# A two-layer attention trunk on one core: the last output tile in two halves, and six fp32 low parts moved between GpSimd and VectorE

## The chip, the core and the metric

The kernel runs on one core of a Trainium2 chip. The core has five engines with a queue each, worked off in order: TensorE (PE in the profile; its weight loads are PEld), VectorE (DVE), ScalarE (ACT), GpSimd (POOL) and SyncE (SP), which here issues the transfers. The metric is the device time of one execution in microseconds; the time of a kernel is the median of its runs.

## The reference

Two layers of one trunk, d_model 1024, on 512 latent tokens and 256 context tokens, in fp32:

```python
def _layer(x, ctx, ...):
    hx = _rmsnorm(x, norm_g) * (1.0 + scale_x) + shift_x      # the same for the context
    a_k, a_v, b_k, b_v, a_q, b_q, a_z, b_z, g_a, g_b = _split(hx @ w_in, SPLIT_SIZES)
    a_att = _na_latent(qa, ka, va, cka, cva, rpb, rows)       # 8 heads, 8 x 16 window + all context
    b_att = _gqa_latent(qb, k_all, v_all)                     # 8 query heads, 2 key heads, all tokens
    out_x = _merge(...)
    return x + gate_x * out_x, ctx                            # layer 0 updates ctx in the same way

def _merge(a_att, b_att, a_z, b_z, g_a, g_b, w_o_a, w_o_b, w_out):
    o_a = (a_att * jax.nn.silu(a_z)) @ w_o_a
    o_b = (b_att * jax.nn.silu(b_z)) @ w_o_b
    merged = jax.nn.sigmoid(g_a) * o_a + jax.nn.sigmoid(g_b) * o_b
    return merged @ w_out
```

`qa`, `ka`, `qb`, `kb` are the normalised (and, for b, rotated) queries and keys of 64 per head. Only the 512 latent tokens of layer 1 are returned, so layer 0 works on 768 tokens throughout and layer 1 on 512 wherever the context is not read.

## The kernel before

**Products in three matmuls.** Each fp32 operand is split into a high part (the value rounded to the format fp32r) and a low part (the value minus its high part, again in fp32r). A product is then three matmuls of 128 rows and up to 512 columns (`mm3`, L351 to L353: high x high, high x low, low x high). The high parts are casts on ScalarE (`whi`, `gah`), the low parts subtractions on VectorE or GpSimd (`wlo`, `gal`). Weights come by DMA from HBM in tiles 128x512 (`raw`) and are split as they come, by `load_w` (L324 makes `wlo`) or `load_w2` (L338). Which engine makes the low part of weight tile k is a rule that the caller hands in; the usual one is

```python
    mix_lo = lambda k: V if k % 2 == 1 else G
```

with V for VectorE and G for GpSimd.

**Stages of a layer.** After the normalisation the keys, the values (`load_w(W, C_AV, ...)`, L621) and the queries of branch a are projected, tile by tile of 128 tokens, with `tok_proj` (PSUM tiles `psx`); the keys' tiles are normalised after it: sums of squares (`ss`, L415, VectorE), their scale (`rsa`, `rsb`, L285 and L287, GpSimd), the scaled tile (`y`, L419, VectorE), and four transposes of it by TensorE (L431). Then come the two attentions, first the windowed one (a), then the grouped one (b). A block of attention b runs as a pipeline over the heads: scores (`pss`, L718 and L719, TensorE), row maximum (`mx`, L955, VectorE), exponential (ScalarE), reciprocal and scaling by it (`r`, `p`, L653 to L659, VectorE and GpSimd), transposes of the probabilities (`pst`, L669, TensorE), their high and low parts (`pth` L672, ScalarE; `ptl` L673, VectorE), the product with the values (`psv`, L972 and L973, TensorE) and the head's output (`ho`, L682, VectorE).

**Filling.** Softmax would leave TensorE waiting, so pieces of other projections are placed between the steps of attention: the gates' pieces (stored through ScalarE's `zt`, L516, as `gs`), and, as soon as branch a is through, its output projection, `o_chunks("a", ...)`. Such a piece is 12 matmuls into one PSUM buffer `psf`, after which VectorE folds it into the gate tile `tg` (L592). Its operand is the gated tile of branch a (`za`, attention times SiLU). Its split into `gah` and `gal` is made by `hilo` in four parts, at the first filling piece of that projection:

```python
        def hilo(src, dst, fs):
            sv = src.rearrange("p (f n) -> p f n", f=4)
            for f in fs:
                S.copy(R(dst[0][:, f, :ntok]), sv[:, f, :ntok])
                G.tensor_tensor(R(dst[1][:, f, :ntok]), sv[:, f, :ntok], dst[0][:, f, :ntok], ALU.subtract)
```

Line L557 is the cast and L558 the subtraction; a part is 128x768 in layer 0 and 128x512 in layer 1. `prepare` (L579) calls it for branch a.

**The end.** Both branches are merged (`mh`, `ml`: high and low part of the merged tile), and the last projection runs in two halves of 512 output columns, each over four (layer 1) tiles of 128 tokens, 24 matmuls a tile. `evac_o` (L1036) then multiplies the tile by the gate (`t`, L1039, from PSUM), adds it to the residual (`xt`, L1041), both on VectorE, and in layer 1 sends the 256 KB to HBM.

**What sets the order.** The program is written stage by stage, and a scheduler that simulates engines with costs of its own orders the instructions on each engine before the kernel is built; on the chip each engine then keeps that order. PSUM has eight buffers: in attention b one `psf`, two `pst`, one `psv` and two `pss` of two banks. Nothing that the change touches has an order written by hand, except the values' weights of layer 0, where the rule was VectorE alone already.

Of the kernel before, what the change touches and what calls it, by code (L numbers as in the profile page):

```python
# [8 lines left out]
F32 = mybir.dt.float32  # L9
# [49 lines left out]
def R(ap):  # L59
    return ap.bitcast(F32R)  # L60
# [7 lines left out]
def hybrid_kernel(es: ExitStack, tc, x, ctx, cvec, w_ada, w_ada0, small, gvec, w_in, w_o_a, w_o_b, w_out,  # L68
# [13 lines left out]
    def nm(s):  # L82
        uid[0] += 1
        return f"{s}_{uid[0]}"
# [405 lines left out]
    def layer(l, hx, nxt, mid):  # L490
# [60 lines left out]
        def hilo_tiles(name):  # L551
            return [big(name + part).rearrange("p (f n) -> p f n", f=4) for part in "hl"]

        def hilo(src, dst, fs):
            sv = src.rearrange("p (f n) -> p f n", f=4)
            for f in fs:
                S.copy(R(dst[0][:, f, :ntok]), sv[:, f, :ntok])  # L557
                G.tensor_tensor(R(dst[1][:, f, :ntok]), sv[:, f, :ntok], dst[0][:, f, :ntok], ALU.subtract)  # L558

        def load_tg(c):  # L560
            nc.sync.dma_start(tg[c].rearrange("p (f n) -> p f n", f=4)[:, :, :ntok], gs[c][:, :, :ntok])
# [17 lines left out]
        def prepare():  # L579

            gated["a"] = hilo_tiles("ga")
            hilo(za, gated["a"], range(4))
            for c in (0, 2):
                tg[c] = big("tg")
                load_tg(c)
# [32 lines left out]
        per_bg = -(-len(bg) // (2 + qt))  # L618
        va = [big("va0"), big("va1")]
        at = len(nc.cur_bb.bb.instructions)  # L620
        w = load_w(W, C_AV, 512, KT, (lambda k: V) if first else mix_lo)  # L621
        if first:
            in_program_order((ON_DVE, ON_ACT), nc.cur_bb.bb.instructions[at:], start_last)
        for t in range(6):
# [370 lines left out]
        with tc.tile_pool(name=f"mrg{l}", bufs=1, reuse_waits="tile") as mp:  # L995
# [37 lines left out]
            for n in range(2):  # L1033
                w = load_w(w_out[l], 512 * n, 512, KT, mix_lo)

                def evac_o(t, ps, n=n):  # L1036
                    cs = slice(512 * n, 512 * n + 512)
                    t1 = mp.tile([128, 512], F32, tag="t1", name=nm("t1"), bufs=2)
                    V.tensor_tensor(t1, ps, gv[:, 0 if t < 4 else 1, cs], ALU.mult)  # L1039
                    xt = xts[t]  # L1040
                    V.tensor_tensor(xt[:, cs], xt[:, cs], t1, ALU.add)  # L1041
                    if not first:
                        nc.sync.dma_start(o_lat[16 * t:16 * t + 16][:, :, cs], xt[:, cs])
                    elif n == 1:
                        if t < 4:
                            nc.sync.dma_start(xs1[128 * t:128 * t + 128, :], xt)
                        late.append(lambda: make_hx(1, t, xt, nxt(), mp))
                late = []
                for t in range(nt):
                    tok_proj(w, 512, a_m, t, evac_o)  # L1050
                    run(bg, per_bg)
                    run(late, len(late) - 1)
                run(late, len(late))
# [186 lines left out]
```

## Time and profile before

| | |
|---|---|
| median of 3 runs | 1148.73 us (1148.03 to 1149.26) |
| the profiled execution | 1149.07 us, of which the span is 1147.0 us |
| TensorE busy | 1123.5 us, 98% of the span |
| VectorE busy | 818.3 us, 71% |
| ScalarE busy | 580.3 us, 51% |
| GpSimd busy | 483.0 us, 42% |
| DMA | 118 GB/s on average |

The first line is the metric. The second is the one execution that was traced: its span runs from the first to the last record, and all starts and durations of rows are counted from its beginning. A busy time is a sum over the records of an engine. A row of the timeline gives start, duration, engine, line, operation, output and inputs, shape, the count of equal neighbours that were drawn together, and in brackets the idle time of the engine before it and what ended it. The first filling piece of branch a's output projection stands at about 480 us in layer 0 and 1005 us in layer 1, the values' weights of layer 1 at about 693 us.

### The profile page before, as it was taken

The page shows a single profiled execution, that of the slowest core. Times are in us where ns is not written, and L with a number is a line of the kernel's source. Part 1 is how long each engine was busy: PE and PEld are TensorE (multiplying, and loading weights), DVE is VectorE, ACT ScalarE, POOL GpSimd, SP SyncE. Part 2 cuts the span into 40 slices and gives each one's busy share as a digit, 9 for nine tenths or more (in the row PEclk, how much of TensorE's full clock was granted, in tenths as well). Part 3 has the DMA queues.
Part 4 walks back from the last instruction along what each step waited for, and adds up shares of the span by engine and source line. Part 5 has one row for each costly group of instructions (what it writes and reads, how often), then busy time and mean ns, then how long its engine had stood idle before and what let it go on. Part 6 is the DMA issues. An engine that isn't in the chain of part 4 may idle for free.

```text
span 1147.0 us, 17434 instructions
## 1 busy us (share of the span) xinstructions
PE 1123.5 (98%) x6136; PEld 949.2 (83%) x6136; DVE 818.3 (71%) x1533; ACT 580.3 (51%) x1185; POOL 483.0 (42%) x449
## 2 busy tenths in 40 slices
PE   7999999999999999999999999999999999999998
PEld 5788888888988888888788787888888888887786
DVE  6777688997454786697588755469787665898563
ACT  6553366655433565665330355336666355766421
POOL 1073355453374343453411227345554664465311
PEclk9999999999999999999999999999999999999999
DMA  9645311333322232451434424633332333152143
GB/s 370 232 127 156 90 51 60 105 110 111 106 101 89 95 103 92 92 221 38 149 127 130 151 70 122 193 89 115 97 113 74 111 102 101 65 176 90 61 133 92
DMA packets 89695, 135.08 MB, mean 118 GB/s; under 512 B 10789, under 2 KB 52745, under 8 KB 88969
## 3 DMA queue, kind: packets, MB, share of 16 engines
q1 hardware_dynamic: 89328, 133.87, 36.8%
q8 instruction: 48, 0.79, 0.3%
q14 instruction: 39, 0.31, 0.1%
q10 hardware_dynamic: 280, 0.12, 0.0%
HBM read 116.63 MB, written 17.32 MB: 117 GB/s over the span
## 4 chain that ended last, share of the span: by engine, by line
PE 80%; DVE 7%; DMA 4%; issue 3%; ACT 3%; POOL 2%; SPq 0%; POOLq 0%; ACTq 0%; DVEq 0%
PE psx L353 12%; PE psx L352 12%; PE psx L351 11%; PE psf L351 9%; PE psf L352 9%; PE psf L353 9%; PE pst L669 4%; DMA raw<-in_w_in_dram 2%; PE pss L718 2%; PE pss L719 2%; PE psv L973 2%; PE psv L972 1%; PE pss L795 1%; PE pst L431 1%; DMA rawb<-in_w_ada_dram 1%
## 5 line engine op out<-in xcount | busy, mean ns | idle before, releaser
L673 DVE TENSOR_TENSOR ptl<-pst,pth 128x512 fp32r<-128x512 f32 (+1 forms) x176 | 115.9, 671 | 46.4 <-ACT pth L672 45.4
L672 ACT CAST pth<-pst 128x512 fp32r<-128x512 f32 (+1 forms) x176 | 99.3, 577 | 86.7 <-PE pst L669 55.8
L338 POOL TENSOR_TENSOR wlo<-raw,whi 128x512 fp32r<-128x512 f32 x68 | 95.6, 1409 | 105.1 <-ACT whi L336 83.9
L351 PE MATMUL psf<-hx,whi 128*128 128x512 f32 (+1 forms) x368 | 139.2, 378 | 0.6 <-ACT zt L516 0.6
L352 PE MATMUL psf<-hx,whi 128*128 128x512 f32 (+1 forms) x368 | 138.2, 375 | 0.0
L353 PE MATMUL psf<-hx,wlo 128*128 128x512 f32 (+1 forms) x368 | 137.8, 374 | 0.0
L351 PE MATMUL psx<-whi,hx 128*128 128x512 f32 (+1 forms) x368 | 137.6, 375 | 0.0
L353 PE MATMUL psx<-whi,hx 128*128 128x512 f32 (+1 forms) x368 | 135.9, 369 | 0.1
L352 PE MATMUL psx<-wlo,hx 128*128 128x512 f32 (+1 forms) x368 | 135.7, 369 | 0.0
L336 ACT CAST whi<-raw 128x512 fp32r<-128x512 f32 x136 | 82.7, 621 | 51.6 <-DMA raw<-in_w_in_dram 35.6
L321 ACT CAST whi<-raw 128x512 fp32r<-128x512 f32 x88 | 53.9, 623 | 99.6 <-PE psx L353 38.1
L669 PE MATMUL pst<-ident,p 128*128 128x128 f32 x640 | 99.9, 272 | 1.4 <-DVE ptl L673 0.8
L324 POOL TENSOR_TENSOR wlo<-raw,whi 128x512 fp32r<-128x512 f32 x36 | 50.9, 1416 | 110.0 <-ACT whi L321 74.6
L338 DVE TENSOR_TENSOR wlo<-raw,whi 128x512 fp32r<-128x512 f32 x68 | 68.6, 1010 | 28.1 <-ACT whi L336 27.2
L669 PEld LDWEIGHTS pst<-ident,p 128*128 128x128 f32 x640 | 77.8, 140 | 13.0 <-DVE ptl L673 1.3
L658 POOL TENSOR_SCALAR r<-r 128x1 f32<-128x1 f32 x64 | 22.4, 350 | 152.2 <-DVE r L653 145.2
L659 POOL TENSOR_TENSOR p<-p,r 128x512 f32<-128x512 f32 (+1 forms) x64 | 84.2, 1316 | 5.1
L353 PEld LDWEIGHTS psx<-whi,hx 128*128 128x128 f32 x368 | 69.4, 189 | 12.6 <-DVE hx L1137 1.0
L351 PEld LDWEIGHTS psx<-whi,hx 128*128 128x128 f32 x368 | 69.5, 189 | 12.4 <-issue 0.8
L353 PEld LDWEIGHTS psf<-hx,wlo 128*128 128x128 f32 x368 | 69.4, 188 | 11.8
L351 PEld LDWEIGHTS psf<-hx,whi 128*128 128x128 f32 x368 | 69.4, 189 | 11.4 <-ACT zt L516 0.8
L352 PEld LDWEIGHTS psx<-wlo,hx 128*128 128x128 f32 x368 | 69.5, 189 | 10.8
(252 smaller groups left out, 3056.0 us busy)
## 6 DMA issues: line engine op xcount, KB each, us to landing
raw<-in_w_in_dram SPq DMA_DIRECT2D x168, 256.0 KB, 2.9
rawb<-in_w_ada_dram SPq DMA_DIRECT2D x64, 256.0 KB, 2.9
gs<-zt SPq DMA_DIRECT2D x32, 256.0 KB, 2.1
raw<-in_w_out_dram SPq DMA_DIRECT2D x32, 256.0 KB, 2.9
tg<-gs SPq DMA_DIRECT2D x4, 1536.0 KB, 6.8
rawx<-in_w_ada_dram SPq DMA_DIRECT2D x8, 512.0 KB, 7.9
raw<-in_w_o_a_dram SPq DMA_DIRECT2D x16, 256.0 KB, 2.8
raw<-in_w_o_b_dram SPq DMA_DIRECT2D x16, 256.0 KB, 2.8
```

The costliest lines, as they stand in the source:

```text
L321: S.copy(hi[:, :n], raw[:, :n])
L324: e.tensor_tensor(lo[:, :n], raw[:, :n], F(hi[:, :n]), ALU.subtract)
L336: S.copy(hi, raw)
L338: lo_eng(i).tensor_tensor(lo, raw, F(hi), ALU.subtract)
L351: T.matmul(ps, lhs[0], rhs[0], start=first, stop=False)
L352: T.matmul(ps, lhs[0], rhs[1], start=False, stop=False)
L353: T.matmul(ps, lhs[1], rhs[0], start=False, stop=last)
L659: G.tensor_tensor(p[:, c0:c1], p[:, c0:c1], r[:, i:i + 1].to_broadcast([128, c1 - c0]), ALU.mult)
L669: T.transpose(pt[:, c0:c0 + 128], src, ident)
L672: S.copy(hi[:, n0:n1], pt[:, n0:n1])
L673: V.tensor_tensor(lo[:, n0:n1], pt[:, n0:n1], F(hi[:, n0:n1]), ALU.subtract)
L718: T.matmul(ps[:, c0:c0 + n], q, sl(kh), start=True, stop=False)
```

## The change

Three edits:

- `hilo` takes a list of engines and deals the four subtractions out by turns. Only branch a's call hands one in, (VectorE, GpSimd): in each layer parts 0 and 2 of the gated tile's low half go to VectorE, parts 1 and 3 stay on GpSimd. Branch b's calls are as before.
- The values' weights of layer 1 have all eight low parts on VectorE; four of them were on GpSimd.
- The last token tile of the last half of layer 1's last projection is computed in two parts of 256 columns, with a PSUM buffer, a multiply, an add and a transfer each.

```diff
--- before.py
+++ after.py
@@ -551,11 +551,11 @@
         def hilo_tiles(name):
             return [big(name + part).rearrange("p (f n) -> p f n", f=4) for part in "hl"]
 
-        def hilo(src, dst, fs):
+        def hilo(src, dst, fs, on=(G,)):
             sv = src.rearrange("p (f n) -> p f n", f=4)
             for f in fs:
                 S.copy(R(dst[0][:, f, :ntok]), sv[:, f, :ntok])
-                G.tensor_tensor(R(dst[1][:, f, :ntok]), sv[:, f, :ntok], dst[0][:, f, :ntok], ALU.subtract)
+                on[f % len(on)].tensor_tensor(R(dst[1][:, f, :ntok]), sv[:, f, :ntok], dst[0][:, f, :ntok], ALU.subtract)
 
         def load_tg(c):
             nc.sync.dma_start(tg[c].rearrange("p (f n) -> p f n", f=4)[:, :, :ntok], gs[c][:, :, :ntok])
@@ -579,7 +579,7 @@
         def prepare():
 
             gated["a"] = hilo_tiles("ga")
-            hilo(za, gated["a"], range(4))
+            hilo(za, gated["a"], range(4), (V, G))
             for c in (0, 2):
                 tg[c] = big("tg")
                 load_tg(c)
@@ -618,7 +618,7 @@
         per_bg = -(-len(bg) // (2 + qt))
         va = [big("va0"), big("va1")]
         at = len(nc.cur_bb.bb.instructions)
-        w = load_w(W, C_AV, 512, KT, (lambda k: V) if first else mix_lo)
+        w = load_w(W, C_AV, 512, KT, lambda k: V)
         if first:
             in_program_order((ON_DVE, ON_ACT), nc.cur_bb.bb.instructions[at:], start_last)
         for t in range(6):
@@ -1033,9 +1033,9 @@
             for n in range(2):
                 w = load_w(w_out[l], 512 * n, 512, KT, mix_lo)
 
-                def evac_o(t, ps, n=n):
-                    cs = slice(512 * n, 512 * n + 512)
-                    t1 = mp.tile([128, 512], F32, tag="t1", name=nm("t1"), bufs=2)
+                def evac_o(t, ps, n=n, c=(0, 512)):
+                    cs = slice(512 * n + c[0], 512 * n + c[1])
+                    t1 = mp.tile([128, 512], F32, tag="t1", name=nm("t1"), bufs=2)[:, :c[1] - c[0]]
                     V.tensor_tensor(t1, ps, gv[:, 0 if t < 4 else 1, cs], ALU.mult)
                     xt = xts[t]
                     V.tensor_tensor(xt[:, cs], xt[:, cs], t1, ALU.add)
@@ -1047,6 +1047,12 @@
                         late.append(lambda: make_hx(1, t, xt, nxt(), mp))
                 late = []
                 for t in range(nt):
+                    if not first and n == 1 and t == nt - 1:
+                        for c in ((0, 256), (256, 512)):
+                            ps = psw(256)
+                            tok_mm(ps, [[a[:, c[0]:c[1]] for a in x] for x in w], 256, a_m, t, 0, KT)
+                            evac_o(t, ps, c=c)
+                        break
                     tok_proj(w, 512, a_m, t, evac_o)
                     run(bg, per_bg)
                     run(late, len(late) - 1)
```

The edits name engines and a shape; the scheduler orders anew. Three places show what came of it. Numbers behind a name tell tiles of the same name apart; a + stands ahead of a row that is new at its place, a - ahead of one that left it.

VectorE, layer 0, at the first gated tile (`gal_1249`). `ptl` are the low parts of probabilities, `wlo_1307` a low part of weights:

```order
 L673 TENSOR_TENSOR ptl_1226_5535<-pst_1224_5529,pth_1225_5534 128x512
 L673 TENSOR_TENSOR ptl_1229_5546<-pst_1227_5540,pth_1228_5545 128x512
+L558 TENSOR_TENSOR gal_1249_5608<-za_230_1097,gah_1248_5607 128x768 x2
 L338 TENSOR_TENSOR wlo_1307_5843<-raw_1305_5839,whi_1306_5841 128x512
 L673 TENSOR_TENSOR ptl_1232_5557<-pst_1230_5551,pth_1231_5556 128x512
```

Two subtractions of 128x768 now stand ahead of `wlo_1307`, after two `ptl` of the running head.

VectorE a few rows on; `tg_1250` is the gate tile, folded with the first pieces `psf_1252` and `psf_1253`:

```order
 L673 TENSOR_TENSOR ptl_1235_5568<-pst_1233_5562,pth_1234_5567 128x512
+L592 SCALAR_TENSOR_TENSOR tg_1250_5617<-tg_1250_5617,psf_1252_5621 128x512
 L673 TENSOR_TENSOR ptl_1239_5583<-pst_1237_5577,pth_1238_5582 128x512
 L955 TENSOR_REDUCE mx_1266_5697<-pss_1264_5691 128x1
 L955 TENSOR_REDUCE mx_1270_5709<-pss_1268_5703 128x1
+L682 TENSOR_TENSOR ho_1236_5573<-psv_1217_5506,ho_1236_5573 64x512
+L673 TENSOR_TENSOR ptl_1279_5737<-pst_1277_5731,pth_1278_5736 128x512
+L592 SCALAR_TENSOR_TENSOR tg_1250_5617<-tg_1250_5617,psf_1253_5635 128x256
 L653 RECIPROCAL r_1267_5699<-r_1267_5699 128x1
-L592 SCALAR_TENSOR_TENSOR tg_1250_5617<-tg_1250_5617,psf_1252_5621 128x512
+L731 TENSOR_REDUCE mx_1273_5721<-pss_1272_5716 128x2
+L653 RECIPROCAL r_1271_5711<-r_1271_5711 128x1
```

The fold moved up, ahead of the reciprocals and maxima (`r`, `mx`) that it followed.

VectorE, layer 1, at the keys' norms; `wlo_1724` to `wlo_1733` belong to the values' weights, `ss8` and `y` to the norms of the keys' tiles:

```order
+L324 TENSOR_TENSOR wlo_1724_7801<-raw_1722_7797,whi_1723_7799 128x512
 L415 TENSOR_REDUCE ss8_1682_7587<-sq_1681_7585 128x8
 L415 TENSOR_REDUCE ss8_1688_7622<-sq_1687_7620 128x8
 L324 TENSOR_TENSOR wlo_1727_7807<-raw_1725_7803,whi_1726_7805 128x512
+L324 TENSOR_TENSOR wlo_1730_7813<-raw_1728_7809,whi_1729_7811 128x512
 L415 TENSOR_REDUCE ss8_1694_7657<-sq_1693_7655 128x8
 L415 TENSOR_REDUCE ss8_1701_7698<-sq_1700_7696 128x8
 L419 TENSOR_TENSOR y_1680_7584<-psx_1679_7559,rsb_1684_7591 128x512
+L324 TENSOR_TENSOR wlo_1733_7819<-raw_1731_7815,whi_1732_7817 128x512
 L415 TENSOR_REDUCE ss8_1708_7739<-sq_1707_7737 128x8
+L419 TENSOR_TENSOR y_1686_7619<-psx_1685_7594,rsb_1690_7626 128x512
```

A `wlo` now precedes the first two sums of squares and another the next two, both ahead of the first scaled tile `y_1680`.

GpSimd at the same place; `rsa` and `rsb` are the two steps of the norms' scale:

```order
 L287 TENSOR_TENSOR rsb_1648_7477<-rsa_1647_7475,ehalf_108 128x1
-L324 TENSOR_TENSOR wlo_1724_7801<-raw_1722_7797,whi_1723_7799 128x512
 L285 TENSOR_SCALAR rsa_1683_7589<-ss8_1682_7587 128x8
 L287 TENSOR_TENSOR rsb_1684_7591<-rsa_1683_7589,ehalf_108 128x8
 L285 TENSOR_SCALAR rsa_1689_7624<-ss8_1688_7622 128x8
-L324 TENSOR_TENSOR wlo_1730_7813<-raw_1728_7809,whi_1729_7811 128x512
+L287 TENSOR_TENSOR rsb_1690_7626<-rsa_1689_7624,ehalf_108 128x8
 L285 TENSOR_SCALAR rsa_1695_7659<-ss8_1694_7657 128x8
-L287 TENSOR_TENSOR rsb_1690_7626<-rsa_1689_7624,ehalf_108 128x8
```

The two subtractions are gone, and the second `rsb` moves up behind its own `rsa`.

TensorE in layer 1, the tail of attention b: first before, from the last of four transposes into `pst_2647` on. `psf_2710` is a piece of branch a's output projection, and these are the first seven of its 12 matmuls:

```order
L669 MATMUL pst_2647_11516<-ident_90,p_2595_11332 128x128
L351 MATMUL psf_2710_11767<-gah_2576_11259,whi_2665_11591 128x512
L352 MATMUL psf_2710_11767<-gal_2577_11260,whi_2665_11591 128x512
L353 MATMUL psf_2710_11767<-gah_2576_11259,wlo_2666_11593 128x512
L351 MATMUL psf_2710_11767<-gah_2576_11259,whi_2665_11591 128x512
L352 MATMUL psf_2710_11767<-gal_2577_11260,whi_2665_11591 128x512
L353 MATMUL psf_2710_11767<-gah_2576_11259,wlo_2666_11593 128x512
L351 MATMUL psf_2710_11767<-gah_2576_11259,whi_2668_11597 128x512
```

The same place after the change; `psf_2751` is the next piece, of branch b's projection, and `pss_2684` the last scores of attention b:

```order
L669 MATMUL pst_2647_11516<-ident_90,p_2595_11332 128x128
L351 MATMUL psf_2751_11903<-gbh_2713_11785,whi_2738_11879 128x512
L352 MATMUL psf_2751_11903<-gbl_2714_11786,whi_2738_11879 128x512
L353 MATMUL psf_2751_11903<-gbh_2713_11785,wlo_2739_11881 128x512
L351 MATMUL psf_2751_11903<-gbh_2713_11785,whi_2738_11879 128x512
L718 MATMUL pss_2684_11655<-gk_2198_9743,qs_2671_11615 128x512
L719 MATMUL pss_2684_11655<-gk_2198_9743,qs_2671_11615 128x512
L718 MATMUL pss_2684_11655<-gk_2198_9743,qs_2671_11615 128x256
L719 MATMUL pss_2684_11655<-gk_2198_9743,qs_2671_11615 128x256
```

Branch a's piece has moved ahead of this place, four matmuls of a later piece stand here instead, and the scores `pss_2684` follow directly.

VectorE at the same place; `mx`, `r`, `ptl` and `ho` belong to the last two heads, `wlo_2766` to the weights of a later projection:

```order
-L592 SCALAR_TENSOR_TENSOR tg_2579_11271<-tg_2579_11271,psf_2709_11753 128x512
+L592 SCALAR_TENSOR_TENSOR tg_2579_11271<-tg_2579_11271,psf_2710_11767 128x512
+L955 TENSOR_REDUCE mx_2678_11636<-pss_2676_11630 128x1
+L338 TENSOR_TENSOR wlo_2766_11993<-raw_2764_11989,whi_2765_11991 128x512
 L673 TENSOR_TENSOR ptl_2646_11511<-pst_2644_11505,pth_2645_11510 128x512
-L955 TENSOR_REDUCE mx_2678_11636<-pss_2676_11630 128x1
 L955 TENSOR_REDUCE mx_2682_11649<-pss_2680_11643 128x1
+L653 RECIPROCAL r_2679_11638<-r_2679_11638 128x1
 L682 TENSOR_TENSOR ho_2617_11407<-psv_2598_11340,ho_2617_11407 64x512
 L673 TENSOR_TENSOR ptl_2649_11522<-pst_2647_11516,pth_2648_11521 128x512
-L653 RECIPROCAL r_2679_11638<-r_2679_11638 128x1
+L955 TENSOR_REDUCE mx_2686_11661<-pss_2684_11655 128x1
```

Ahead of `ptl_2646` now stand the fold of the later piece, the maximum `mx_2678` and the weights' `wlo_2766`.

## The prediction

> **What bounds the kernel now.** I read the page's busy shares first, then busy time by stage for the stages that the edits touch, then the waits and the timeline inside them. The first line below is from the page, the others are stretches of the span; their columns are the length, then busy time and instruction count of each engine, the granted clock, the DMA share and GB/s.
>
> ```profile
> PE 1123.5 (98%) x6136; PEld 949.2 (83%) x6136; DVE 818.3 (71%) x1533; ACT 580.3 (51%) x1185; POOL 483.0 (42%) x449
> 480.00:504.00 24.00, 21.71 (x135) 18.47 (x134) 19.76 (x32) 16.63 (x33) 17.46 (x13) 1.00 0.84 315
> 690.00:712.00 22.00, 21.21 (x101) 17.09 (x100) 12.77 (x21) 13.38 (x26) 17.48 (x17) 1.00 0.39 116
> 1000.00:1048.00 48.00, 47.70 (x250) 39.62 (x250) 44.04 (x66) 32.51 (x63) 28.32 (x26) 1.00 0.43 148
> 1048.00:1080.00 32.00, 29.24 (x155) 21.98 (x155) 22.38 (x34) 17.94 (x33) 13.29 (x13) 1.00 0.16 50
> ```
>
> TensorE works 98% of the span, at a granted clock of 1.00, so an edit gains only where TensorE waits. In the four stretches it is short of the full time by 2.3, 0.8, 0.3 and 2.8 us: 6.2 us in all is what the two moves of work could give at most by these rows (short waits that hide behind the modelled end of a matmul come on top). In the third stretch VectorE is busy 44 of 48 us: it is nearly a second bound there, and what the change does there is put work on VectorE.
>
> **The end of the kernel.** The last tile's 24 matmuls of 512 columns become 48 of 256, with two multiplies, two adds and two output transfers.
>
> ```profile
> 1136.18 0.39 PE L352 MATMUL psx<-wlo,mh 128*128 128x512 f32 x1
> 1141.17 0.39 PE L353 MATMUL psx<-whi,ml 128*128 128x512 f32 x1
> 1141.60 0.69 DVE L1039 TENSOR_TENSOR t<-psx,gate 128x512 f32<-128x512 f32 x1 [3.80 <-PE psx L353]
> 1142.32 0.69 DVE L1041 TENSOR_TENSOR xt<-xt,t 128x512 f32<-128x512 f32 x1
> ...
> 478.96 0.28 PE L351 MATMUL psf<-hx,whi 128*128 128x256 f32 x1
> 481.72 0.28 PE L353 MATMUL psf<-hx,wlo 128*128 128x256 f32 x1
> ...
> L592 DVE SCALAR_TENSOR_TENSOR tg<-tg,psf 128x256 f32<-128x256 f32 x8 | 3.3, 409 | 0.4 <-PE psf L353 0.4
> L1008 DVE TENSOR_TENSOR tg<-tg,tg 128x256 f32<-128x256 f32 x8 | 3.9, 486 | 0.1
> ...
> DMA to landing us min/median/max: 2.8/2.8/3.3
> zs<-zt SPq DMA_DIRECT2D x4, 128.0 KB, 1.9
> gs<-zt SPq DMA_DIRECT2D x16, 128.0 KB, 2.9
> ```
>
> From the first row to the second there are 22 steps of 512 columns: 4.99 / 22 = 0.227 us each. The 256-column rows of another stage (24 matmuls, 23 steps) give 2.76 / 23 = 0.120 us. So 24 x 0.227 = 5.45 us become 48 x 0.120 = 5.76 us: +0.31 us on the path, and with the start moved by 45 steps and the shorter last matmul (0.28 for 0.39) its end is also 0.3 us later. After it the multiply (0.69) and the add (0.69) work on half the columns: 0.41 by the L592 row, which reads PSUM as the multiply does, and 0.41 to 0.49 for the add. That takes off 0.28 and about 0.24. The first part's multiply, add and issue lie beside the second part's 2.76 us of matmuls, which hide them; the extra issue on SP delays nobody, since nothing else is queued there. The last transfer carries 128 KB: 256 KB of output landed in 2.8 us, other 128 KB stores in 1.9 to 2.9. That bounds it at -0.9 to +0.1; I take -0.1, since the same stores of 256 KB are not slower than those of 128 KB. Sum: +0.31 - 0.28 - 0.24 - 0.1 = -0.3 us (-1.1 to +0.2).
>
> **Layer 0, the first gated tile.** Of four subtractions 128x768 on GpSimd, the first and third go to VectorE.
>
> ```profile
> 479.09 1.29 DVE L673 TENSOR_TENSOR ptl<-pst,pth 128x512 fp32r<-128x512 f32 x2 [0.33 <-ACT pth L672]
> 480.48 3.04 ACT L557 CAST gah<-za 128x768 fp32r<-128x768 f32 x4
> 481.70 8.00 POOL L558 TENSOR_TENSOR gal<-za,gah 128x768 fp32r<-128x768 f32 x4
> 484.06 1.80 DVE L338 TENSOR_TENSOR wlo<-raw,whi 128x512 fp32r<-128x512 f32 x1 [3.69 <-ACT whi L336]
> 484.88 0.50 PE L351 MATMUL psf<-gah,whi 128*128 128x512 f32 x1 [1.07 <-ACT zt L516]
> 485.79 0.68 DVE L673 TENSOR_TENSOR ptl<-pst,pth 128x512 fp32r<-128x512 f32 x1
> 495.40 0.63 PE L669 MATMUL pst<-ident,p 128*128 128x128 f32 x4 [0.56 <-DVE r L653]
> 501.54 0.39 PE L351 MATMUL psf<-gah,whi 128*128 128x256 f32 x1 [0.66 <-DVE tg L592]
> ```
>
> ScalarE makes the four high parts from 480.48, 0.76 us each; VectorE is free from 480.4 to 484.06, so the first can start at 481.3 and the third at 482.8. VectorE's own price for 128x768 is in no row. The low end is the `wlo` subtraction of 128x512 at 0.68 us (row of 695.18 below) times 1.5, 1.0 us; the high end is the same subtraction at 1.80 us while GpSimd runs its gated parts, times 1.5, 2.7 us. I take 1.5, between them, as GpSimd now runs only two. Then VectorE comes to its next `wlo` some 0.3 us late and is about 0.5 us late behind it. On the other side GpSimd is done at about 486 instead of 489.7, and TensorE can run the whole first piece (12 matmuls) at once from 484.88; that start does not move, it waits for ScalarE's `zt`. What can go is the later 0.56 and 0.66 us of waiting, for VectorE's `r` and `tg`, since `tg` now stands ahead of the softmax scalings. But VectorE has no gap from 484 to 501, and whatever it lost comes back at its next `ptl`. From both sides: -1.2 to +2; I take 0.
>
> Here a rule weighs against the change. The Trainium skill ("SBUF — State Buffer", "Who interferes with whom") says that a VectorE instruction with two SBUF inputs and a GpSimd instruction that reads SBUF exclude each other for the whole instruction. The trace agrees as far as it goes: `wlo` has two SBUF inputs and took 1.80 us beside GpSimd, `ptl`, whose one input is PSUM, took 0.68 beside the same GpSimd work. By the rule the halves do not run side by side, and this term would be up to the +2 of the range and not 0.
>
> **Layer 1, the values' weights.** Four low parts 128x512 move from GpSimd to VectorE. The keys' norms stand in both queues there.
>
> ```profile
> 693.98 1.28 DVE L415 TENSOR_REDUCE ss<-sq 128x8 f32<-128x512 f32 x2 [0.85 <-ACT sq L413]
> 695.18 0.68 DVE L324 TENSOR_TENSOR wlo<-raw,whi 128x512 fp32r<-128x512 f32 x1
> 695.25 2.15 POOL L287 TENSOR_TENSOR rsb<-rsa,ehalf 128x8 f32<-128x8 f32 x1
> 697.43 0.69 DVE L419 TENSOR_TENSOR y<-psx,rsb 128x512 f32<-128x512 f32 x1 [0.15 <-POOL rsb L287]
> 697.81 1.29 POOL L324 TENSOR_TENSOR wlo<-raw,whi 128x512 fp32r<-128x512 f32 x1
> 698.27 0.63 PE L431 MATMUL pst<-ident,y 128*128 128x128 f32 x4 [0.71 <-ACT sq L413]
> 701.21 0.69 DVE L419 TENSOR_TENSOR y<-psx,rsb 128x512 f32<-128x512 f32 x1 [0.47 <-POOL rsb L287]
> 701.96 0.65 PE L431 MATMUL pst<-ident,y 128*128 128x128 f32 x4
> ```
>
> TensorE waits 0.71 us for the first normalised tile `y`, made at 697.43 as soon as `rsb` is done, and again about 0.24 us for the second. In the new order VectorE has a `wlo` (0.68) ahead of the first two sums, so `rsb` starts no earlier although GpSimd lost its own subtraction, and another ahead of the next two sums: from 693.5, 0.68 + 1.28 + 0.68 + 0.68 + 1.28 = 4.6 us, so the first `y` starts at 698.2 instead of 697.43: +0.8. The second `rsb` no longer has GpSimd's 1.29 us subtraction (697.81) ahead of it, so the second wait, 0.24, goes. Net +0.5 us. Nothing hides it: six tiles fill the PSUM buffers, and the next projection cannot start before `y` is read. Low end: if VectorE's order is as late as I think only by its waits, -0.9 (both waits gone); high end +0.8. I take +0.5. Later weights have room: the low part that TensorE needed at 707.7 is now made by about 702.5.
>
> **Layer 1, the gated tile and the tail of attention.** Two subtractions 128x512 move here too.
>
> ```profile
> 1004.86 3.23 DVE L338 TENSOR_TENSOR wlo<-raw,whi 128x512 fp32r<-128x512 f32 x2 [1.72 <-ACT whi L336]
> 1005.93 5.82 POOL L558 TENSOR_TENSOR gal<-za,gah 128x512 fp32r<-128x512 f32 x4
> 1049.66 0.39 PE L718 MATMUL pss<-gk,qs 128*128 128x512 f32 x1
> 1055.42 0.95 DVE L955 TENSOR_REDUCE mx<-pss 128x1 f32<-128x768 f32 x1
> 1056.29 1.75 DVE L338 TENSOR_TENSOR wlo<-raw,whi 128x512 fp32r<-128x512 f32 x1
> 1058.69 0.50 PE L973 MATMUL psv<-ptl,vb 128*128 128x512 f32 x1 [1.54 <-DVE ptl L673]
> 1059.62 0.49 PE L973 MATMUL psv<-ptl,vb 128*128 128x512 f32 x1
> 1061.78 0.39 PE L973 MATMUL psv<-ptl,vb 128*128 128x512 f32 x1
> ```
>
> VectorE pays 2 x 0.7 to 2 x 1.6 us (its rows alone and beside GpSimd) for them, with 1.7 us free just ahead of 1004.86: about 1 us late behind them. The larger effect is the order. The low parts are there sooner, so every projection piece of 12 matmuls stands one place earlier on TensorE, ahead of attention work; at the last scores but two (`pss_2676`, ending at 1049.66 in the profile) TensorE has done 12 x 0.227 = 2.7 us more. What follows there is paced by VectorE: three maxima (0.95), `wlo` (0.7 to 1.75), five subtractions or head outputs (0.69), a scaling and reciprocals, with waits 9.5 us until the fourth value step of that head, against 1059.62 - 1049.66 = 10.0 us before. So that step is 2.7 - 0.5 = 2.2 us later, with five more filling matmuls done. Two steps on, those five lie behind in both: 1061.78 - 1059.62 = 2.2 us before, some 1.0 us after. Net 2.2 - 1.2 = +1.0 us; I take off 0.1 for small waits that the earlier pieces cover. +0.9, from -1.7 (the 1.54 us wait at 1058.69 goes and nothing follows) to +2.7 (the whole piece lost to a tail without filling).
>
> **Sum.** -0.3 + 0 + 0.5 + 0.9 = +1.1 us. The profiled execution took 1149.07 us (span 1147.0), 0.34 above the median of the runs, 1148.73; the difference is put on the median: 1149.8 us.
>
> **Rivals.** *The waits simply go* (faster): VectorE takes the parts into its gaps at 0.7 to 1.0 us each, and TensorE's waits at 495.4, 501.5 and 1058.7 (0.56 + 0.66 + 1.54) vanish with the end's -0.6: -3.4 us, 1145.3. For it: TensorE is the bound and these are its waits; against it: VectorE has 4 us of slack in the 48 before the last wait. *The engines exclude each other* (slower): if every moved subtraction waits for a GpSimd one, VectorE is late by 2.4 us behind the pair in layer 0 (two GpSimd parts of 1.9 instead of its gap, less 1.4) and 3 us behind that in layer 1 (`wlo` at 1011 instead of 1008); of the 5.4 us about 2 are caught in VectorE's slack: with the other terms +4, 1152.8. It decides from some 1.2 us per moved part on. This is what the Trainium skill's rule would make of it ("SBUF — State Buffer", "Who interferes with whom"); the row of 3.23 us for two `wlo` speaks for it. *All of it hidden*: only the end counts, the new order costs nothing and gains nothing: 1148.4.
>
> **How the numbers follow.** My sum 0.36, all hidden 0.24, waits go 0.23, exclusion 0.17. No change that can be told is within 0.2%, 2.3 us, of 1148.73, which holds the first two. With a little of the outer cases inside and of the sum outside: faster 0.24, same 0.55, slower 0.21. The likeliest cases alone lie in 1147 to 1151; with the outer ones the range is 1145.0 to 1152.6, which leaves out about one in ten on each side.
>
> **What would show it.** In the new profile: the last add ends 0.2 us earlier against the first matmul of its tile; the gated subtractions on VectorE take about 1.5 us (1.0: the faster rival; 2.5: exclusion); the wait for the first `y` in layer 1 is 1.5 us instead of 0.71 and the second is gone; between the last scores but two and the end of the last head's values TensorE idles more than the 2.8 us of the old last stretch. I am wrong if that stretch shrinks, or if VectorE finishes its `wlo` in layer 0 as early as before.

## The result, and the profile after

The changed kernel takes 1151.44 us (median of 11 runs, 1150.68 to 1152.24) against 1148.56 (11 runs, 1148.03 to 1149.61): 1.0024 times as long, with a 95% interval of 1.0014 to 1.0033. It is slower by 2.9 us. The profiled execution took 1151.03 us, its span is 1149.2.

The four stretches of after, with the columns of those shown of before:

```profile
480.00:504.00 24.00, 21.75 (x135) 18.48 (x133) 22.45 (x34) 16.36 (x33) 14.83 (x11) 1.00 0.84 315
690.00:712.00 22.00, 21.05 (x101) 17.24 (x100) 16.60 (x27) 15.20 (x30) 14.37 (x14) 1.00 0.49 141
1000.00:1048.00 48.00, 44.72 (x229) 36.15 (x228) 44.99 (x64) 28.14 (x55) 25.39 (x22) 1.00 0.42 144
1048.00:1080.00 32.00, 29.91 (x161) 22.52 (x159) 22.06 (x36) 20.50 (x38) 14.66 (x13) 1.00 0.12 40
```

TensorE lacks 2.25 us of full time in the first stretch (2.3 before), 0.95 in the second (0.8), 3.3 in the third (0.3) and 2.1 in the fourth (2.8). The loss sits in the third, the one in which VectorE was nearly a second bound.

To see where the time went, TensorE's records of the two traces were matched by operation and tile; the table gives by how much a record of after starts later than its partner, as a median over 20 us:

| place in the trace of before | after minus before, us |
|---|---|
| 460 to 480 | -0.26 |
| 520 to 540 (behind layer 0's gated tile) | -0.21 |
| 680 to 700 | -0.14 |
| 720 to 740 (behind the values' weights) | -0.25 |
| 1000 (ahead of layer 1's gated tile) | -0.95 |
| 1060 to 1080 (behind it) | +3.06 |
| 1120 to 1140 | +3.08 |
| end of the span | +2.2 |

So layer 0 cost 0.05 us, the values' weights gave 0.1, layer 1's gated tile cost 4.0, and the end gave 0.9. (The 0.55 between 940 and 960 is no effect of the change: it stands in the traces of all the kernels compared below, 0.5 to 0.7 us, so it belongs to the one execution of before that was traced.)

What happened at 1001 to 1011 us, on VectorE, GpSimd and TensorE. The bracket is the idle time ahead and what ended it:

```profile
1001.81 1.87 DVE L656 TENSOR_SCALAR p<-p,r 128x768 f32<-128x768 f32 x1
1003.60 3.48 DVE L558 TENSOR_TENSOR gal<-za,gah 128x512 fp32r<-128x512 f32 x2
1007.01 3.47 DVE L338 TENSOR_TENSOR wlo<-raw,whi 128x512 fp32r<-128x512 f32 x2
1010.40 0.68 DVE L673 TENSOR_TENSOR ptl<-pst,pth 128x512 fp32r<-128x512 f32 x1
1001.80 1.46 POOL L659 TENSOR_TENSOR p<-p,r 128x768 f32<-128x768 f32 x1
1003.34 1.50 POOL L683 TENSOR_TENSOR zb<-zb,ho 64x512 f32<-64x512 f32 x1
1004.92 3.31 POOL L558 TENSOR_TENSOR gal<-za,gah 128x512 fp32r<-128x512 f32 x2
1008.20 1.74 POOL L338 TENSOR_TENSOR wlo<-raw,whi 128x512 fp32r<-128x512 f32 x1
1011.14 0.50 PE L973 MATMUL psv<-ptl,vb 128*128 128x512 f32 x1 [1.32 <-DVE ptl L673]
```

The two moved subtractions take 1.74 us each on VectorE and the two weight parts behind them 1.74 each, where the same operation took 0.68 at 695.18 in the trace of before. These two weight parts were slow before too (3.23 us for both at 1004.86, the row in the prediction), so what is new is the 3.48 us of the subtractions, of which 1.72 fit into the idle time ahead of that row. GpSimd is busy from 1001.80 to 1009.94 without a gap worth naming. The `ptl` behind that block starts at 1010.40; before it was 1008.01, on a time scale 0.95 us later. It is 3.3 us late, and TensorE waits for it.

The end of the kernel: the first matmul of the last tile that both traces show, then VectorE's last two instructions and the landing of the output transfers (minimum, median, maximum):

```profile
1139.26 0.28 PE L352 MATMUL psx<-wlo,mh 128*128 128x256 f32 x1
1144.97 0.42 DVE L1039 TENSOR_TENSOR t<-psx,gate 128x256 f32<-128x256 f32 x1 [1.87 <-PE psx L353]
1145.43 0.42 DVE L1041 TENSOR_TENSOR xt<-xt,t 128x256 f32<-128x256 f32 x1
DMA to landing us min/median/max: 2.3/2.8/3.2
```

From 1139.26 to the last add's end, 1145.85, it is 6.59 us; before, from 1136.18 to 1143.01, 6.83. The shorter transfers land in 2.3 us; the span's remainder behind the last add is 3.35 us instead of 3.99.

### The profile page after: what moved, and what is told of

It reads as the page before. It is cut to its first block, busy times and chain, and to the rows that moved or that the text cites. A ratio compares the mean times of both kernels' runs of the same rounds, so it can differ in the third digit from the quotient of the medians.

```text
span 1149.2 us, 17495 instructions
## 1 busy us (share of the span) xinstructions
PE 1124.5 (98%) x6160; PEld 950.5 (83%) x6160; DVE 828.3 (72%) x1543; ACT 580.2 (50%) x1185; POOL 473.7 (41%) x441
## 4 chain that ended last, share of the span: by engine, by line
PE 83%; DVE 8%; DMA 3%; issue 3%; POOL 2%; ACT 1%; SPq 0%; POOLq 0%; ACTq 0%; DVEq 0%
PE psx L351 12%; PE psx L353 12%; PE psx L352 12%; PE psf L351 9%; PE psf L352 9%; PE psf L353 9%; PE pst L669 5%; PE pss L718 2%; PE pss L719 2%; PE psv L973 2%; PE psv L972 2%; PE pss L795 1%; PE pst L431 1%; DMA raw<-in_w_in_dram 1%; DVE ptl L673 1%
## 5 line engine op out<-in xcount | busy, mean ns | idle before, releaser
L338 POOL TENSOR_TENSOR wlo<-raw,whi 128x512 fp32r<-128x512 f32 x68 | 97.3, 1434 | 104.5 <-ACT whi L336 84.3
L324 POOL TENSOR_TENSOR wlo<-raw,whi 128x512 fp32r<-128x512 f32 x32 | 45.5, 1422 | 104.1 <-ACT whi L321 87.6
```

What stands on the lines that cost most here:

```text
L324: e.tensor_tensor(lo[:, :n], raw[:, :n], F(hi[:, :n]), ALU.subtract)
L338: lo_eng(i).tensor_tensor(lo, raw, F(hi), ALU.subtract)
```

## Experiments

Every kernel below was timed in turn with the kernel before on the same chip; differences are between medians of one batch, the intervals are those of the ratio.

**The three edits apart.** Each run is the kernel before with a part of the change: `tail_only` has the last of the three edits, `values_only` the second, `gal_only` the first, `tail_values` the last two.

```diff
 tail_only:    evac_o and the loop over t as in the change, all else as before
 values_only:  -w = load_w(W, C_AV, 512, KT, (lambda k: V) if first else mix_lo)
               +w = load_w(W, C_AV, 512, KT, lambda k: V)
 gal_only:     -hilo(za, gated["a"], range(4))
               +hilo(za, gated["a"], range(4), (V, G))
```

> Before with the last tile in two parts alone. Theory A (the loss is VectorE's lateness behind the moved subtractions in layer 1, everything else is small): the end gains what the two traces show there, 0.85 us: 1147.7, and the stretch from 1000 to 1080 us stays as before. Theory B (the terms of the prediction, -0.3 / 0 / +0.5 / +0.9, with a common drift on top): 1148.3. Theory C (the three edits matter only together, through one new order): within 0.3 us of 1148.56.

> Before with the gated tile's subtractions dealt to VectorE and GpSimd in both layers, nothing else. Theory A: +4.0 us (the shift between the traces from 1000 to 1064 us) and nothing in layer 0: 1152.6; TensorE waits over 1 us for ptl near 1011 us, and VectorE's two low parts of weights end there 2 to 3 us later than before. Theory B: +0.9, 1149.5. Theory C: within 0.5 us of 1148.56.

> Before with the low parts of layer 1's values' weights all on VectorE, nothing else. Theory A: the first normalised tile comes 0.2 us later and the second wait of 0.24 us is gone: 0 to -0.1 us, 1148.5. Theory B: +0.5, 1149.1, with a first wait of 1.5 us. Theory C: within 0.3 us of 1148.56.

> The changed kernel with the gated tile's subtractions all back on GpSimd: the end and the values' weights alone. Theory A: -0.85 - 0.1 us, 1147.6, faster than before by 0.08%. Theory B: -0.3 + 0.5, 1148.8. Theory C: between the two kernels, about 1150.

Measured against 1148.47: `tail_only` 1147.59 (-0.9; ratio 0.9990, 0.9981 to 0.9999), `gal_only` 1151.32 (+2.85; 1.0023, 1.0014 to 1.0032), `values_only` 1148.83 (+0.4; 1.0000, 0.9991 to 1.0009), `tail_values` 1147.98 (-0.5; 0.9993, 0.9984 to 1.0002). Theory A holds for the end, and it has the gated tile as the loss. It gave the gated tile 4.0 us and that was 1.2 too much, and in the trace of `gal_only` TensorE does not wait over 1 us for `ptl` near 1011 us, as it said; its longest wait there is 0.71 us, for the fold `tg` (last row below). The values' weights can't be told from no change. Theory C is out: the parts add up to +2.3, the whole is +2.9, and the intervals are wider than the rest.

`gal_only` has, in layer 1's attention, the order of the changed kernel on every engine. Yet its VectorE block is less late: its `ptl` starts at 1010.0 on the scale of before, not at 1011.35. VectorE's scaling and its two subtractions, GpSimd's scaling, and TensorE's wait:

```profile
1001.47 0.65 DVE L656 TENSOR_SCALAR p<-p,r 128x768 f32<-128x768 f32 x1
1002.04 3.66 DVE L558 TENSOR_TENSOR gal<-za,gah 128x512 fp32r<-128x512 f32 x2
1001.67 1.78 POOL L659 TENSOR_TENSOR p<-p,r 128x768 f32<-128x768 f32 x1
1015.02 0.50 PE L351 MATMUL psf<-gah,whi 128*128 128x512 f32 x1 [0.71 <-DVE tg L592]
```

Here VectorE's scaling starts 0.2 us ahead of GpSimd's and takes 0.65, and GpSimd's takes 1.78. In the changed kernel's trace GpSimd's started 0.01 us ahead and took 1.46, and VectorE's took 1.87. So in those two executions the first to start ran at its own speed and the other waited, and 1.2 us of the 4.0 hang on 0.2 us of phase. That is read from one execution each. In the twelve other traces VectorE's scaling comes first, as here, so the slow case was seen in the one traced execution of the changed kernel alone. The medians show less of it: the changed kernel lies 3.4 us above `tail_values`, `gal_only` 2.85 above before.

**Which layer.** `gal_l0` and `gal_l1` move the two subtractions in one layer alone.

```diff
 gal_l0:  +hilo(za, gated["a"], range(4), (V, G) if first else (G,))
 gal_l1:  +hilo(za, gated["a"], range(4), (G,) if first else (V, G))
```

> Before with the two gated subtractions of layer 1 alone on VectorE. If the loss is all in layer 1 (theory A): all of the +2.85 us that both layers' subtractions cost, 1151.3. If layer 0 has a share that the shift of the traces hides: half of it, 1149.9.

> Before with the two gated subtractions of layer 0 alone on VectorE. Theory A: the shift between the traces around 480 to 520 us is 0.05 us, so 1148.5, within 0.3. If layer 0 has a share of the loss: 1149.9.

Against 1148.62: `gal_l1` 1151.67 (+3.05; 1.0028, 1.0016 to 1.0039), `gal_l0` 1148.63 (0.0; 1.0001, 0.9993 to 1.0010). The whole loss is layer 1's. Why layer 0 pays nothing, its trace shows: first VectorE in the trace of before, two scalings `p`, the first beside GpSimd's four subtractions and the second beside GpSimd's own scaling,

```profile
486.64 1.34 DVE L656 TENSOR_SCALAR p<-p,r 128x768 f32<-128x768 f32 x1
491.86 1.23 DVE L656 TENSOR_SCALAR p<-p,r 128x768 f32<-128x768 f32 x1
```

and the same place after:

```profile
481.08 1.22 DVE L558 TENSOR_TENSOR gal<-za,gah 128x768 fp32r<-128x768 f32 x1 [0.97 <-ACT gah L557]
482.55 2.25 DVE L558 TENSOR_TENSOR gal<-za,gah 128x768 fp32r<-128x768 f32 x1 [0.25 <-ACT gah L557]
484.73 2.34 DVE L338 TENSOR_TENSOR wlo<-raw,whi 128x512 fp32r<-128x512 f32 x1
487.84 0.80 DVE L656 TENSOR_SCALAR p<-p,r 128x768 f32<-128x768 f32 x1
494.64 0.60 DVE L656 TENSOR_SCALAR p<-p,r 128x768 f32<-128x768 f32 x1
499.72 0.63 PE L669 MATMUL pst<-ident,p 128*128 128x128 f32 x4 [1.17 <-DVE ptl L673]
```

VectorE takes 3.5 us for the two subtractions, most of it in the 3.7 us that it stood idle there before (the row of 484.06 in the prediction), and 0.5 more for the weight part. GpSimd is through earlier, and the two scalings take 1.2 us less. Of TensorE's waits of 0.56 and 0.66 us none is left, and one of 1.17 at 499.72 has come in their place.

**Time or order.** The scheduler laid out layer 1's attention anew, so the loss can come from VectorE's time or from the order. Two kernels hold one of them fixed. A table gives the order of the instructions of that stage (some 480 on TensorE, 125 on VectorE, 78 on ScalarE, 28 on GpSimd), and a dependency of the kind NoSync ties each to the one ahead of it on its engine:

```diff
+        made = {i.name: i for i in nc.cur_bb.bb.instructions}
+        for names in ORDER.values():
+            names = [f"I-{n}" for n in names.split()]
+            for a, b in zip(names, names[1:]):
+                tc.add_manual_dep(made[b], a, ... NoSync ..., reason="program order")
```

> The two gated subtractions of layer 1 on VectorE, at the place in its queue where the changed kernel has them, but every other instruction of layer 1's attention on every engine in the order of before. Theory T (the loss is VectorE's time: its two subtractions and its next two weight parts take 1.7 us each beside GpSimd, and the ptl behind them comes over 2 us late): TensorE waits 2 us or more near 1009 us, 1150.5 to 1151.5, as much as the kernel that moves the subtractions alone. Theory O (the loss is the new order, in which the filling is used up earlier): within 0.4 us of before, 1148.5.

> All four gated subtractions of layer 1 on GpSimd as before, but every other instruction of layer 1's attention on every engine in the order that came of moving two of them. Theory T: VectorE is as early as before, so little is lost: 1148.2 to 1149. Theory O: the loss of the moved kernel comes with the order, +2 to +2.9 us, 1150.5 to 1151.4; besides, TensorE may wait for the low parts that GpSimd finishes 2.5 us later, which would be seen as waits for gal.

Against 1148.62: `old_order_moved` 1150.77 (+2.15; 1.0019, 1.0011 to 1.0028), `new_order_unmoved` 1149.42 (+0.8; 1.0008, 0.9999 to 1.0016). With the order of before, VectorE's time alone costs 2.15, the larger part of the 3.05 of `gal_l1`: theory T, though TensorE's wait for `ptl` is 1.37 us and not 2 or more. The other 0.9 is what `gal_l1` lost beyond `old_order_moved`, and the intervals of the two overlap. First `old_order_moved`: the subtractions, the two weight parts, `ptl`, and TensorE's wait for it,

```profile
1002.19 3.66 DVE L558 TENSOR_TENSOR gal<-za,gah 128x512 fp32r<-128x512 f32 x2
1005.78 3.47 DVE L338 TENSOR_TENSOR wlo<-raw,whi 128x512 fp32r<-128x512 f32 x2
1009.16 0.68 DVE L673 TENSOR_TENSOR ptl<-pst,pth 128x512 fp32r<-128x512 f32 x1
1009.90 0.51 PE L973 MATMUL psv<-ptl,vb 128*128 128x512 f32 x1 [1.37 <-DVE ptl L673]
```

then `new_order_unmoved`, the weight parts and `ptl` as early as before, a wait of TensorE for `gal`, and in the tail the same matmul that waited 1.54 us at 1058.69 before:

```profile
1004.45 3.25 DVE L338 TENSOR_TENSOR wlo<-raw,whi 128x512 fp32r<-128x512 f32 x2 [1.71 <-ACT whi L336]
1007.61 0.68 DVE L673 TENSOR_TENSOR ptl<-pst,pth 128x512 fp32r<-128x512 f32 x1
1010.14 0.50 PE L352 MATMUL psf<-gal,whi 128*128 128x512 f32 x1 [0.28 <-POOL gal L558]
1058.78 0.51 PE L973 MATMUL psv<-ptl,vb 128*128 128x512 f32 x1 [0.25 <-DVE ptl L673]
```

Its +0.8, whose interval just reaches no change, is no price for the new order in `gal_l1`, although 2.15 and 0.8 add up to nearly 3.05. Here GpSimd still makes all four parts and TensorE reads them earlier, so it waits for them, as the expectation had warned: the steps to the matmuls at 1008.90 and 1010.14 take 0.53 and 0.67 us instead of 0.23, together 0.74 us too much, and TensorE's shift over the whole stage in this trace is 0.7. In the trace of `gal_l1` no step waits for `gal` at that place. The tail costs nothing more in the new order: in the 32 us from 1047.6 us on TensorE lacks 2.25 us of full time here, against 2.8 from 1048 us on before. What the new order costs beside the moved subtractions, and where, stays open.

**Why VectorE's subtractions take 1.7 us.** `old_order_allv` gives VectorE all four subtractions of layer 1; `pool_parts_on_act` leaves it two and puts copies on ScalarE in the place of GpSimd's two; these two low parts then hold the whole value, so only its time counts. Both keep the order of before.

```diff
 old_order_allv:     +hilo(za, gated["a"], range(4), (G,) if first else (V,))
 pool_parts_on_act:  +if on == (V, G) and f % 2 == 1:
                     +    S.copy(R(dst[1][:, f, :ntok]), sv[:, f, :ntok])
                     +    continue
```

> As old_order_moved (every other instruction of layer 1's attention in the order of before), but all four gated subtractions of layer 1 on VectorE, GpSimd has none. Theory E (a VectorE subtraction with two SBUF inputs and a GpSimd instruction with SBUF inputs exclude each other; alone they take 0.66 and 1.30 us): VectorE's block of six subtractions takes 6 x 0.66 plus GpSimd's other work beside it (the scaling that still runs, one 64-row product and one weight part, up to 1.3 us each), 6 to 7 us, and ends at 1008 to 1009.5 on the time scale of before, earlier than in old_order_moved although VectorE does two more: the wait for ptl shrinks, 1148.6 to 1150. Theory V (a subtraction between SBUF tiles costs VectorE 1.7 us at this place whoever else works): 6 x 1.75 = 10.5 us, the block ends 3.5 us later than in old_order_moved: 1153.5 or more.

> As old_order_moved, but GpSimd's two gated subtractions of layer 1 are replaced by copies on ScalarE, in a gap of 1.9 us there; those two low parts then hold a copy of the value itself, so this is for the time alone. Theory E (VectorE's subtractions are slow because GpSimd reads SBUF beside them): the two weight parts on VectorE then meet one GpSimd subtraction and not three, take about 2.4 us instead of 3.5, and ptl comes 1.1 us earlier: 1149.4 to 1149.9. If VectorE's 1.7 us have another cause: 1150.8 as in old_order_moved.

`old_order_allv` took 1151.12 against 1148.99 (+2.1; 1.0018, 1.0009 to 1.0027), `pool_parts_on_act` 1149.14 against 1148.86 (+0.3; 1.0003, 0.9994 to 1.0012). VectorE and GpSimd in `old_order_allv`:

```profile
1003.33 5.96 DVE L558 TENSOR_TENSOR gal<-za,gah 128x512 fp32r<-128x512 f32 x4
1009.22 1.28 DVE L338 TENSOR_TENSOR wlo<-raw,whi 128x512 fp32r<-128x512 f32 x2
1004.81 1.63 POOL L683 TENSOR_TENSOR zb<-zb,ho 64x512 f32<-64x512 f32 x1
1006.52 1.62 POOL L338 TENSOR_TENSOR wlo<-raw,whi 128x512 fp32r<-128x512 f32 x1
```

and in `pool_parts_on_act`, whose lines stand three further down:

```profile
1003.91 3.66 DVE L561 TENSOR_TENSOR gal<-za,gah 128x512 fp32r<-128x512 f32 x2
1007.49 2.38 DVE L338 TENSOR_TENSOR wlo<-raw,whi 128x512 fp32r<-128x512 f32 x2
1007.10 1.62 POOL L338 TENSOR_TENSOR wlo<-raw,whi 128x512 fp32r<-128x512 f32 x1
```

GpSimd ends at 1008.14 in the first and 1008.72 in the second. Weight parts that VectorE makes behind that take 0.64 us each (1009.22), those beside it 1.74 (the second row of `old_order_moved`); the pair of which one stands beside it takes 2.38 = 1.74 + 0.64. This is what theory E says; theory V's 1153.5 is out. E's own sum for `old_order_allv` was short: the block took 7.2 us and not 6 to 7, its `ptl` started 0.1 us later than in `old_order_moved` on a common scale and not earlier, and the time was 1.1 us above its range. For `pool_parts_on_act` the time is 0.3 us below E's range, with `ptl` 1.1 us earlier, as E says.

**What stands behind it.** `ptl_first` is `old_order_moved` with the two weight parts put further back on VectorE, behind the third `ptl` and the first `tg`.

```diff
 VectorE:  -gal gal wlo wlo ptl mx ptl mx r ptl     r p ptl mx tg     ...
           +gal gal         ptl mx ptl mx r ptl wlo r p ptl mx tg wlo ...
```

> As old_order_moved (two gated subtractions of layer 1 on VectorE, all else in the order of before), but VectorE's two weight parts, which stood between the subtractions and the ptl, come later: one behind the third ptl, one behind the first tg. If the loss is the lateness of ptl behind that block (theory T), ptl comes at 1006 to 1007 us on the scale of before, earlier than the 1008.0 there, TensorE's wait of 1.5 us goes, and what stays is VectorE's extra work being caught up: 1148.5 to 1149.4. If the loss comes from the sum of VectorE's work in the stretch, whatever its order: 1150.8 as in old_order_moved.

1149.68 against 1148.86 (+0.8; 1.0008, 0.9999 to 1.0017).

```profile
1003.52 3.66 DVE L558 TENSOR_TENSOR gal<-za,gah 128x512 fp32r<-128x512 f32 x2
1007.53 0.69 DVE L673 TENSOR_TENSOR ptl<-pst,pth 128x512 fp32r<-128x512 f32 x1 [0.34 <-PE pst L669]
1012.08 1.03 DVE L338 TENSOR_TENSOR wlo<-raw,whi 128x512 fp32r<-128x512 f32 x1
1015.81 0.69 DVE L338 TENSOR_TENSOR wlo<-raw,whi 128x512 fp32r<-128x512 f32 x1
```

The first `ptl` is early, as expected, and 1.3 of the 2.15 us are gone. But this does not tell the two cases of the expectation apart, since VectorE's time did not stay the same. The subtractions are as slow as ever (3.66), while the weight parts, now beside less of GpSimd's work or none, take 1.03 and 0.69 us, 1.75 less than the 3.47 ahead of `ptl`.

The traces speak for the sum of VectorE's time. Behind the block VectorE has next to no gap (two of 0.3 us between 1008 and 1030 us in the trace of before), so what it is late by stays with it. TensorE pays for it either at the first `ptl` or, at the latest, at the fold `tg` some 20 us on. Its wait there, first in the trace of before, then in `ptl_first`:

```profile
1028.24 0.50 PE L351 MATMUL psf<-gah,whi 128*128 128x512 f32 x1 [0.25 <-DVE tg L592]
1029.26 0.50 PE L351 MATMUL psf<-gah,whi 128*128 128x512 f32 x1 [0.53 <-DVE tg L592]
```

The table has the kernels that keep the order of before, all on its scale (each trace's shift ahead of this stage taken off): the start of the first `ptl` behind the block, by how much VectorE's records from 1016 to 1030 us are late, TensorE's shift over the stage, and the change of the median.

| kernel | start of `ptl`, us | VectorE late by, us | shift over the stage, us | median, us |
|---|---|---|---|---|
| before | 1008.0 | 0 | 0 | 0 |
| `ptl_first` | 1007.1 | +0.55 | +0.5 | +0.8 |
| `pool_parts_on_act` | 1008.9 | +0.85 | +0.85 | +0.3 |
| `old_order_moved` | 1010.0 | +1.95 | +1.95 | +2.15 |
| `old_order_allv` | 1010.15 | +2.1 | +2.1 | +2.1 |

TensorE's loss is VectorE's lateness in all four traces. (The traced execution of `pool_parts_on_act` was the slowest of its eleven, 1150.71, so its median need not fit its trace.) The start of `ptl` goes with it in three and not in `ptl_first`, where `ptl` is early and the loss falls between 1022 and 1030 us. A kernel with the weight parts behind `ptl` and as slow as ahead of it wasn't run, so that the place in the queue alone gains anything is not shown.

**The cut of the last tile.** `tail_384` cuts at column 384.

```diff
-for c in ((0, 256), (256, 512)):
+for c in ((0, 384), (384, 512)):
```

> tail_only with the last tile cut at column 384 in place of 256, so that only 128 columns stand behind the last matmul. If the time of a step is in proportion to its columns (0.227 and 0.120 us for 512 and 256 give 0.174 for 384 and 0.067 for 128), the 48 matmuls take the same 5.8 us, the multiply and the add lose 0.13 us each and the last transfer some 0.2: 0.4 us under tail_only, 1147.2. If a step of 128 columns takes as long as that of the transposes (0.087), the matmuls take 0.5 us more and nothing is gained: 1147.6 to 1147.8.

1148.48 against 1148.99 (-0.5; 0.9996, 0.9987 to 1.0004): nothing gained over `tail_only`'s -0.9. The first and last complete step of 128 columns, VectorE's last instruction and the landing:

```profile
1140.26 0.27 PE L353 MATMUL psx<-whi,ml 128*128 128x128 f32 x1
1142.60 0.28 PE L353 MATMUL psx<-whi,ml 128*128 128x128 f32 x1
1143.24 0.29 DVE L1041 TENSOR_TENSOR xt<-xt,t 128x128 f32<-128x128 f32 x1
DMA to landing us min/median/max: 2.0/2.8/3.2
```

Between them lie 21 steps in 2.34 us, 0.111 us each: 128 columns cost nearly what 256 do (0.120), more than either case of the expectation. (The 0.087 that it took for a transpose was too low: four transposes take 0.60 us, as in the row of 701.81 below, and one alone 0.27, which leaves 0.11 for a step.) 24 x (0.111 - 0.067) = 1.1 us eat up the 0.4 from the shorter end. The Trainium skill ("TensorE: Matmul & The Clock Gate", "LDWEIGHTS (loading the stationary operand)") gives a weight load the number of its columns over 1.2 as nanoseconds, so 107 ns for 128 as an estimate. The step of 0.111 us is near that figure; that the weight load sets the step is not shown.

Of all kernels run, `tail_only` has the lowest median: it beats the kernel before by 0.1% and the changed one by 0.3%.

## Why the prediction was right and wrong

The time lies in the range (1145.0 to 1152.6), 1.6 us above the forecast of 1149.8, and just beyond the bound of 0.2% inside which most of the chance was placed: slower had 0.21. That the total is so near is in part luck, since the terms missed in opposite directions: the gated tile by 2.15 upwards, the end by 0.6 and the values' weights by up to 0.5 downwards.

**The end**, -0.3: right in kind, a third of the size. VectorE's and TensorE's part was 0.24, as worked out. The landing was put at -0.1, and the 128 KB landed 0.5 us or more earlier; `tail_only` gave -0.9. The transfer's own bounds, -0.9 to +0.1, held that, and a value nearer their low end would have been right. (The +0.2 at the upper end of its sum does not follow from its terms, which give -0.1.)

**Layer 0**, 0: right, and with its reason: what VectorE lost came back at a later `ptl`, TensorE's two waits went and one of about the same size (1.17 against 1.22 in all) came. The price of a subtraction was between its bounds (1.22 and 2.25 against 1.0 to 2.7). Not foreseen was that GpSimd's shorter work would pay part of it back through VectorE's scalings.

**The values' weights**, +0.5: not settled by the times (+0.4, interval -1.0 to +1.0), and by the trace wrong in the step that put the first `wlo` on the path: the row that I quoted shows VectorE idle for 0.85 us just there, and it fits into that. Rows of after, the weight part in the gap, the first `y`, and TensorE's two transposes:

```profile
693.34 0.69 DVE L324 TENSOR_TENSOR wlo<-raw,whi 128x512 fp32r<-128x512 f32 x1 [0.35 <-ACT whi L321]
697.53 0.68 DVE L419 TENSOR_TENSOR y<-psx,rsb 128x512 f32<-128x512 f32 x1
698.35 0.63 PE L431 MATMUL pst<-ident,y 128*128 128x128 f32 x4 [0.95 <-DVE y L419]
701.81 0.60 PE L431 MATMUL pst<-ident,y 128*128 128x128 f32 x4
```

The wait for the first `y` is 0.95 us and not 1.5; the second has gone, as said.

**Layer 1's gated tile**, +0.9 with bounds of -1.7 and +2.7: the failed term; it measured +3.05, above its bounds. Two steps of it failed. The one that it priced, a tail that idles more because a filling piece is used up earlier, +1.0 less 0.1, is not what the runs show: TensorE idles less in the tail in the new order, and the 0.8 us of `new_order_unmoved` are by its trace waits for `gal`, so that the sizes are alike is chance. The other it left without a price: VectorE was called "about 1 us late", from 2 x 0.7 to 2 x 1.6 us less 1.7 us free. It was 2.0 us late in `old_order_moved`, since two subtractions took 3.66 us and the weight parts behind them 3.47 instead of 3.23, and TensorE paid all of it, 1.65 us at the next `ptl` and the rest up to the fold `tg`: +2.15 in the median.

**The rivals.** *Exclusion* had the mechanism: its point of decision, 1.2 us per moved part, was passed (1.7 to 1.8), and its `wlo` at 1011 instead of 1008 is what the trace of after shows, whose pair ends at 1010.5. It was wrong on layer 0, where its 2.4 us were covered, and on the size of the end, so 1152.8 was 1.4 too high. Its +4 does not follow from its terms either: 5.4 less 2, with -0.3 and +0.5, is 3.6. The Trainium skill's rule ("SBUF — State Buffer", "Who interferes with whom") is borne out: a subtraction with two inputs in SBUF on VectorE took 1.74 us beside GpSimd and 0.64 alone. *The waits simply go* and *all hidden* failed in layer 1; the first also counts the end as -0.6, twice the sum's own term.

**What would show it**: "I am wrong if that stretch shrinks" came true. The stretch from 1048 us went from 2.8 us short to 2.1 (2.3 if it is taken 3 us later, as the kernel then runs), so the extra idling in the tail was wrong; the kernel was slower all the same, because the idling came in the stretch ahead of it.

## What to carry to other kernels

Before work is moved from GpSimd to VectorE, look whether GpSimd stays busy beside it: price the moved instruction by rows that have GpSimd at work next to them (here 1.74 us, not 0.64), and so for the instructions that follow it. Then look how far behind it VectorE's queue has no gap: what VectorE is late by there, TensorE paid in these kernels, and in `ptl_first` an early first operand seems only to have moved the place where it did. By the traces what helped there was less time on VectorE: with the two weight parts put where GpSimd was done or nearly so, they took 1.72 us instead of 3.47, and the loss went from 2.15 to 0.8 us.

## What the runs showed of the hardware

- VectorE and GpSimd hold each other up almost wholly. Side by side, a subtraction of SBUF tiles on each takes 1.74 us on VectorE and 1.66 on GpSimd (after, 1007.01 and 1004.92); one after the other they would take 0.64 (`old_order_allv`, 1009.22) + 1.29 (before, 697.81) = 1.93. VectorE's instruction stretches to 2.7 times its length, GpSimd's to 1.3 times.
- A scaling by one number per row, with a single tensor in SBUF, is held up as well: 0.65 us when it started 0.2 us ahead of GpSimd's (`gal_only`), 1.87 when it started 0.01 us behind it (after). The second case was traced once.
- A step of TensorE with 128 columns took 0.111 us (`tail_384`), with 256 columns 0.120 (after): here a cut finer than 256 columns bought no time.
- A 128 KB store of output landed in 2.3 us (after) where 256 KB took 2.8 to 3.3 (before), and one of 64 KB in 2.0 (`tail_384`).
